# A decoder trunk on one core: K handed over behind pinned copies at the seams, one bank's copy into a free place, three of w_out's sets kept as plain sums, and the last product taken pair by pair

## The chip, the cores and the metric

The kernel runs on one core of one Trainium2 chip. Its engines are TensorE (PE, matrix products, with PEld for its weight loads), VectorE (DVE), ScalarE (ACT), GpSimd (POOL) and SyncE (SP, which issues nearly all DMAs). The metric is the time of one execution on the device, in microseconds (us); the median over runs is given. A profiled execution gives the trace, which has its own time.

## The reference

One decoder layer (DEPTH 1, BATCH 1, SEQ 2048, D_MODEL 1024, all float32), whose outputs must be met to float32-like accuracy:

```python
mod = jax.nn.silu(c) @ w_ada[l] + b_ada[l]
shift, scale, gate = jnp.split(mod, 3, axis=-1)
u = x * (1.0 + scale[:, None, :]) + shift[:, None, :]
h = u @ w_in[l]
q, k, v, a_gate, p_in, p_gate, m_a, m_p = jnp.split(h, offsets, axis=-1)
a = sliding_window_sink_attention(q, k, v, sinks[l], bias, mask) * jax.nn.silu(a_gate)
a = a @ w_attn_proj[l]
p = jnp.einsum('bsgc,gcd->bsgd', multiscale_causal_pool(p_in), w_pool_mix[l]).reshape(B, S, POOL_WIDTH)
p = (p * pool_scale[l]) * jax.nn.silu(p_gate)
p = p @ w_pool_proj[l]
y = jax.nn.sigmoid(m_a) * a + jax.nn.sigmoid(m_p) * p
y = (y @ w_out[l]) * (1.0 + gate[:, None, :])
x = layer_norm(DEEPNORM_ALPHA * x + y, ln_gain[l], ln_bias[l])
```

The attention has 16 query heads and 2 key-value heads of 64, a window of 128 and a sink per head; the pool takes causal means over 2, 4, 8 and 16 positions.

## The kernel before

**Products.** Every large matrix product is computed in 2 x 2 blocks with seven block products instead of eight. They are called B11, T1, T2, B21, T3, B22 and T4, after the *set* (the moving operand, 1024 x 512 sums of blocks) that each uses. The weights of a product are blocks of the stationary matrix or sums of them: a `Quad` loads four blocks into the tile `W` (places 0 to 3; place 0 holds A11) and `A22`, and GpSimd forms the sums in place (`sum1`, `mid`, `late`). To keep accuracy, each operand is split into a high and a low part in the matrix engine's 32-bit format, and a product is 12 matmuls of 128x128 by 128x512 (four steps, each of high·high, high·low, low·high). The split is a cast on ScalarE (high) and a subtraction on VectorE (low), `pair_split` for two places of `W`, `half_split` for `A22`; the results lie in the ring `w_set`, which has four places, so that two pair splits fill it.

**Groups and phases.** Two quads make a group. `front` does B11 and T1 of a quad, which accumulate in the banks a and b (`mm` in the trace); `back` does T2 (bank c, `lg`), B21 (into a), T3 (into c), B22 (into b) and T4 (into c), with copies and adds between them: u2 is a copy of a, taken before B21 accumulates there, and is added to c; p5 is a copy of b; then `b = c + p5`. `third(x)` splits the weights of T3 and B22 of quad x, and with `b22_first` (the first group after an attention) both quads' B22 come before T3. Finished banks go to a `consume` of the quad: `take_k` splits K into `kk` by eight alternating copies for each 512 columns (ScalarE high, VectorE low), `gate_quad` applies sigmoids, `attn_quad` and `pool_quad` apply gates and collect `wide` sums and y, and the w_out quads add the residual and normalize rows.

The order in time is: the first gate phase; attention of the first half of the sequence; the second gate phase; attention of the second half; then the "mix", four phases (attention projection and pool projection of each half), and last w_out with LayerNorm rows. In an attention, TensorE works through the heads while the products of the next phase's first quads (`opened`) are woven in, up to T2 of both and B21 of the first. The places where an attention ends and `back` takes over are called the **first seam** (to the second gate phase) and the **second seam** (to the mix). The third place of interest is the change from the last pool phase to w_out.

**What sets the order.** The program is written in one order, and a scheduler places the instructions on each engine; an engine executes its own list in that order. Engine handles named `act`, `dve`, `pe`, `sp`, `pool` are *pinned*: what is issued through them keeps the written order among itself. What is issued through `nc.scalar`, `nc.vector` and so on may be moved by the scheduler. A `tick` comes after every product; `hooks` hang further steps on ticks.

**Sets.** The sets of the next phase are loaded step by step while the present one runs. They lie in DRAM either as *plain sums* (two halves of 512 KB for each set), fetched into a spare buffer and split on arrival (`set_steps`: a fetch, and some ticks later the split, at the ticks of `SPLIT_AT`), or already *split* (four parts, 1 MB for each half), filled straight into place at the ticks of `PLAN`. w_out's sets are made in the second gate phase by `sums_to`, which calls `kept_parts`: a high part `k_hi`, a low part `k_lo` and two writes of 256 KB for each of four row pairs and each set.

Of the kernel before, what the change touches and what calls it, by code (L numbers as in the profile page):

```python
# [19 lines left out]
P = 128  # L20
# [39 lines left out]
def kernel(  # L60
# [49 lines left out]
    def set_store(name):  # L110
        return {n: dp.tile([2, P, 2, CH], F32, name=f"{name}_{n}") for n in set_names}

    def split_store(name):
        return {n: dp.tile([4, P, 2, CH], F32, name=f"{name}_{n}_split") for n in set_names}

    b12_d = dp.tile([2, P, 2, CH], F32, name="b12_d")
    u1_d = split_store("u1")
    wo_d = split_store("wo")
    ain0_d = split_store("ain0")
    ain_d = [set_store(f"ain{s}") for s in range(2)]  # L120
    pin_d = [set_store(f"pin{s}") for s in range(2)]
# [9 lines left out]
    def low(engine, dst, src, hi):  # L131
        engine.tensor_tensor(dst, src, as32(hi), ALU.subtract)  # L132
# [95 lines left out]
    def sums_to(ph, store, i, load, work, b12):  # L228

        b = []  # L230

        def x(r, c):
            return b[r][:, c * CH : (c + 1) * CH]

        def fetch():
            b.extend((ph.spare(), ph.spare()))
            b.reverse()
            for r in (1, 0):
                load(b[r], r)

        def sub(out, a, c):
            return lambda: pool.tensor_tensor(x(*out), x(*a), x(*c), ALU.subtract)

        todo = [(0, fetch), (3, lambda: work(b[0], 0)), (3.5, lambda: work(b[1], 1))]
        todo += [(at, sub(*z)) for at, z in (
            (7.5, ((0, 1), (0, 1), (0, 0))),
            (9, ((1, 1), (1, 1), (0, 1))),
            (10.5, ((1, 0), (1, 0), (1, 1))),
            (12, ((0, 0), (1, 1), (0, 0))),
        )]  # L250
        for at, name, z in (
            (4, "B11", (0, 0)), (4.7, "B12", (0, 1)), (5.4, "B21", (1, 0)), (6.1, "B22", (1, 1)),
            (8.5, "T1", (0, 1)), (10, "T2", (1, 1)), (11.5, "T4", (1, 0)), (13, "T3", (0, 0)),
        ):
            if b12 or name != "B12":
                split, keep = kept_parts(ph, store[name][i], lambda z=z: x(*z))
                todo += [(at, split), (at + 1, keep)]
        return sorted(todo, key=lambda t: t[0])
# [61 lines left out]
    def by_two(t):  # L320
        return t.rearrange("p (a c) -> p a c", a=2)
# [37 lines left out]
        tick()  # L359
        return a, b, None, None  # L360

    def back(ph, grp, opened, nxt, own, tick, b22_first=False):
        st = []
        for q, (a, b, c, w, *copy) in zip(grp, opened):
            p5 = ph.p("p5")
            if w is None:
                c = bank("lg")
                nc.scalar.copy(c, a)
                nc.scalar.copy(p5, b)
                w = pair_split(ph, q.second())[::-1]  # L370
                q.late()
                product(c, w[1], "T2")
            else:
                u2 = copy[0] if copy else ph.p("u2")
                if not copy:
                    nc.scalar.copy(u2, a)
                if c is None:
                    c = bank("lg")
                    product(c, w[1], "T2", True)
                nc.vector.tensor_tensor(c, c, u2, ALU.add)  # L380
                nc.scalar.copy(p5, b)
            tick()
            nc.vector.tensor_tensor(b, c, p5, ALU.add)
            if not copy:
                product(a, w[0], "B21")
            tick()
            q.consume(ph, 0, 0, a)
            st.append((q, b, c, p5))
        w = {}

        def ask(q):

            defer(1, lambda: q.load(ph, own, sp if b22_first else nc.sync, None))
            defer(3, lambda: q.sum1(nc.gpsimd))

# [12 lines left out]
        def with_b22(x):  # L408
            q, b, c, p5 = st[x]
            product(b, w[x][0], "B22")  # L410
            tick()
            q.consume(ph, 0, 1, b)

        if b22_first:
            for x in range(len(st)):
                third(x)
                with_b22(x)
            for x in range(len(st)):
                with_t3(x)
        else:  # L420
            for x in range(len(st)):
                third(x)
                with_t3(x)
                with_b22(x)
        for q in nxt[len(st) :]:
            ask(q)
        for q, b, c, p5 in st:
            w = half_split(ph, q.a22)
            product(c, w, "T4")
            tick()  # L430
            q.consume(ph, 1, 0, c)
# [9 lines left out]
            due.remove(d)  # L441
            d[2]()

    def ring(ph, groups, opened, hooks, nxt, after, b22_first=False):
# [12 lines left out]
        for gi, grp in enumerate(groups):  # L457
            pos[:] = [gi, 0]
            own = gi % 2 == 0 and gi + 1 < len(groups)
            back(ph, grp, opened, (groups + [nxt])[gi + 1], own, tick, b22_first and gi == 0)  # L460
# [24 lines left out]
    def set_steps(ph, store):  # L485


        if store["B11"].shape[0] == 4:
            return [(p, lambda n=n, h=h: fill_set(n, h, store[n])) for p, n, h in PLAN]
        raw, todo = {}, []  # L490

        def fetch(k):
            name, half = PLAN[k][1:]
            raw[k] = ph.spare()
            sp.dma_start(raw[k], store[name][half].rearrange("p a b -> p (a b)"))

        def split(k):
            name, half = PLAN[k][1:]
            split_set(name, 2 * half, by_two(raw[k]), 2, (act, dve))

        for k, at in enumerate(SPLIT_AT):
            if k < 2:
                todo.append((0, lambda k=k: fetch(k)))
            todo.append((at, lambda k=k: split(k)))
            if k + 2 < len(SPLIT_AT):
                todo.append((at, lambda k=k: fetch(k + 2)))
        return todo

    def planned(hooks, ph, store, last, pending={}):
        if last:  # L510
# [146 lines left out]
            low(nc.vector, dst[:, :, kv, HD:], vtp[:, :, kv, :], dst[:, :, kv, 0:HD])  # L657

    def take_k(s, t, kp):
        if s > 0 and t == 0:  # L660
            nc.vector.tensor_copy(kk[:, :, :, 0:P], kk[:, :, :, 2 * CH :])
        c0 = P + t * CH
        for kv in range(2):
            src = kp[kv * HD : kv * HD + HD, :]
            for half in (kv, 1 - kv):
                dst = kk[half * HD : half * HD + HD, kv, :, c0 : c0 + CH]
                nc.scalar.copy(dst[:, 0, :], src)
                low(nc.vector, dst[:, 1, :], src, kk[kv * HD : kv * HD + HD, kv, 0, c0 : c0 + CH])

    def bias_rows():  # L670
        room = cp.tile([P, 4 * D], F32, tag="set_T2", name="head_T2")
# [49 lines left out]
    def attention(ph, s, q0, nxt):  # L721
# [170 lines left out]
        for n in range(N + 5):  # L892
# [96 lines left out]
                    early_lo(x, which)  # L989
            if n in (59, 62):  # L990
                nxt_group[n // 62].mid()
            if n == 64:
                opened[0].append(nxt_group[0].w[:, 0, :])
                act.copy(opened[0][4], opened[0][0])
            for st in range(2):
                if n % U == 3 + 2 * st and (j, st) in sums:
                    pgs[j, st] = ld("pg", gates_d["pg"][s, j, st])
# [116 lines left out]
    def head(ph):  # L1114
# [113 lines left out]
        def second_pair(x):  # L1228

            o, u2 = opened[x], ph.p("u2")  # L1230
            o[2:] = bank("lg"), pair_split(ph, grp[x].second(), act, dve)[::-1], u2
            act.copy(u2, o[0])

        def more(x, name, i0, i1):
            a, b, c, w, _ = opened[x]
# [157 lines left out]
    with Pools("mix", spare=2, p=2, c=5) as ph:  # L1393
# [9 lines left out]
        for i, (groups, store) in enumerate(phases):  # L1403
# [7 lines left out]
            if i + 1 < len(phases):  # L1411
                planned(hooks, ph, phases[i + 1][1], True)
                nxt = phases[i + 1][0][0]
                after = lambda tick, nxt=nxt: [front(ph, q, tick) for q in nxt]
            else:
                for at, row in ((1, 2), (1, 3), (5, 4), (5, 5)):
                    hooks.setdefault((0, at), []).append(lambda row=row: load_z(ph, row))
            if i in (2, 4):
                ta.clear()
            if i == 3:  # L1420
# [8 lines left out]
            opened = ring(ph, groups, opened, hooks, nxt, after, i == 0)  # L1429
# [53 lines left out]
```

## Time and profile before

| | |
|---|---|
| median of 3 runs | 1770.89 us (1770.28 to 1771.1) |
| profiled execution | 1766.12 us |
| its span, first to last instruction | 1764.3 us |
| mean granted TensorE clock | 0.992 |
| instructions | 24983 |
| PE, DVE, ACT, POOL busy | 97%, 68%, 53%, 45% |
| DMA moved | 381.30 MB, mean 216 GB/s |

In a row of the timeline stand: start, duration, engine, line, operation, output<-inputs by name with shapes, count, and in brackets the idle time of that engine before the row and what ended it. A row with a count above one runs from the first of its instructions to the last. In a row of stretches stand the stretch, its length, then busy time and count of PE, PEld, DVE, ACT and POOL, then the granted TensorE clock (1.00 is full), the share of the DMA engines and GB/s. In a row of groups stand the count, the busy time, the mean ns of one and the idle time before. In a row of DMA issues stand the count, the size of each and the median us from issue to landing.

### The profile page before, as it was taken

The numbers are of one execution on the slowest core, as the hardware profiler recorded it, in microseconds if no ns is written. First come the engines' busy times: TensorE is split into PE (matmuls) and PEld (weight loads), VectorE is DVE, ScalarE is ACT, GpSimd is POOL, SyncE is SP. The second block draws the span as 40 slices with busy tenths as digits, with TensorE's granted clock in tenths as the row PEclk, the third lists the DMA queues.
The fourth block names the chain that finished last, engine by engine and source line by source line (L and its number), as shares of the span: only waits on it lengthen the run. The fifth ranks groups of instructions, "written<-read, shape, count | busy, mean of one in ns | idle before, by whom it ended". The sixth has DMA issues, their size and how long they took to land. (4 is left out here: it accounts for less than half of the span.)

```text
span 1764.3 us, 24983 instructions
## 1 busy us (share of the span) xinstructions
PE 1702.9 (97%) x8248; PEld 1428.7 (81%) x8248; DVE 1206.0 (68%) x2180; ACT 931.8 (53%) x1969; POOL 792.7 (45%) x618
## 2 busy tenths in 40 slices
PE   6899999999999998999999999999999989999996
PEld 5688888888888887888788888888888768888785
DVE  5967665655777786766655367777867586765777
ACT  4544444545777775454444377777744333423451
POOL 2145454431356567434434125456762562364542
PEclk9999999999999999999999999999999999999998
DMA  9384767743354567687777634544796585689432
GB/s 365 112 279 179 270 210 273 271 148 132 108 173 146 172 219 294 245 281 254 246 274 262 231 98 132 175 155 149 258 356 225 182 257 182 226 314 384 166 143 99
DMA packets 180609, 381.30 MB, mean 216 GB/s; under 512 B 18800, under 2 KB 39296, under 8 KB 180480
## 3 DMA queue, kind: packets, MB, share of 16 engines
q1 hardware_dynamic: 173696, 363.66, 59.2%
q0 software_dynamic: 3552, 11.56, 1.7%
q10 hardware_dynamic: 3232, 4.49, 0.9%
q8 instruction: 65, 1.06, 0.2%
q14 instruction: 64, 0.52, 0.1%
HBM read 244.35 MB, written 138.44 MB: 217 GB/s over the span
## 5 line engine op out<-in xcount | busy, mean ns | idle before, releaser
L56 PE MATMUL mm<-set_B,w_set 128*128 128x512 f32 x3240 | 801.8, 396 | 17.5 <-DVE w_set L132 8.7
L56 PEld LDWEIGHTS mm<-set_B,w_set 128*128 128x128 f32 x3240 | 604.2, 189 | 147.4 <-DVE w_set L132 15.2
L56 PE MATMUL lg<-set_T,w_set 128*128 128x512 f32 x2088 | 505.9, 392 | 14.0 <-DVE w_set L132 8.6
L56 PEld LDWEIGHTS lg<-set_T,w_set 128*128 128x128 f32 x2088 | 390.8, 188 | 103.7 <-DVE w_set L132 14.0
L132 DVE TENSOR_TENSOR w_set<-W,w_set 128x1024 fp32r<-128x1024 f32 x162 | 224.1, 1383 | 175.7 <-ACT w_set L325 171.4
L325 ACT CAST w_set<-W 128x1024 fp32r<-128x1024 f32 x162 | 169.7, 1049 | 242.4 <-PE mm L56 195.6
L56 PE MATMUL mm<-set_T,w_set 128*128 128x512 f32 x1080 | 266.2, 394 | 0.0
L56 PEld LDWEIGHTS mm<-set_T,w_set 128*128 128x128 f32 x1080 | 201.1, 189 | 41.3
L294 POOL TENSOR_TENSOR W<-W,A 128x512 f32<-128x512 f32 x56 | 82.1, 1466 | 221.7 <-DMA W<-in_win_dram 55.9
L303 POOL TENSOR_TENSOR W<-W 128x512 f32<-128x512 f32 x56 | 80.1, 1431 | 155.5 <-DVE w_set L132 143.9
L56 DVE TENSOR_TENSOR o<-pv,o 64x128 f32<-64x128 f32 x256 | 72.4, 283 | 88.3 <-ACT o L56 85.4
L56 ACT ACTIVATE L<-L,nm 128x257 f32<-128x257 f32 (+1 forms) x256 | 127.2, 498 | 9.3 <-DVE nm L56 3.9
L298 POOL TENSOR_TENSOR W<-W 128x512 f32<-128x512 f32 x56 | 88.1, 1574 | 93.8 <-DVE w_set L132 84.7
L56 DVE CUSTOM_DVE_ANT_0 L<-lg,bt,nsink 128x256 f32<-128x256 f32 (+1 forms) x256 | 111.6, 473 | 5.0 <-PE lg L56 0.8
L299 POOL TENSOR_TENSOR W<-W 128x512 f32<-128x512 f32 x56 | 88.1, 1573 | 37.3 <-DMA W<-in_win_dram 28.1
L56 POOL TENSOR_TENSOR w_set<-W,w_set 128x1024 fp32r<-128x1024 f32 x14 | 33.7, 2405 | 139.6 <-ACT w_set L56 97.0
L56 POOL TENSOR_TENSOR p<-nxt,pg 128x512 f32<-128x512 f32 x32 | 42.0, 1311 | 106.4 <-DVE sm L56 102.8
L56 ACT COPY o<-pv 64x256 f32<-64x256 f32 x128 | 47.3, 370 | 78.1 <-PE pv L56 77.3
L56 DVE TENSOR_TENSOR ptl<-pt,pth 128x512 fp32r<-128x512 f32 (+1 forms) x128 | 85.7, 669 | 1.9 <-ACT pth L56 1.7
L56 DVE TENSOR_TENSOR k_lo<-spare,k_hi 128x512 fp32r<-128x512 f32 x61 | 63.2, 1041 | 28.8 <-ACT k_hi L56 15.0
L56 PE MATMUL lg<-kk,qs 128*128 128x256 f32 (+1 forms) x512 | 80.5, 279 | 0.0
L56 ACT ACTIVATE L<-L,sm 128x256 f32<-128x256 f32 (+1 forms) x128 | 64.3, 502 | 29.4 <-DVE sm L56 29.4
(208 smaller groups left out, 2304.9 us busy)
## 6 DMA issues: line engine op xcount, KB each, us to landing
W<-in_win_dram SPq DMA_DIRECT2D x48, 512.0 KB, 5.3
w_set<-wmix_d SPq DMA_DIRECT2D x32, 512.0 KB, 5.2
W<-in_win_dram SPq DMA_DIRECT2D x34, 256.0 KB, 3.4
A<-in_win_dram SPq DMA_DIRECT2D x34, 256.0 KB, 5.0
ag_d<-sig SPq DMA_DIRECT2D x32, 256.0 KB, 3.3
pg_d<-sig SPq DMA_DIRECT2D x32, 256.0 KB, 3.7
ma_d<-sig SPq DMA_DIRECT2D x32, 256.0 KB, 3.9
mp_d<-sig SPq DMA_DIRECT2D x32, 256.0 KB, 3.8
```

The lines of the kernel that those rows point to most:

```text
L56: return lambda *args, **kw: self.tc.keep_in_program_order(op(*args, **kw))
L132: engine.tensor_tensor(dst, src, as32(hi), ALU.subtract)
L294: e.tensor_tensor(self.w[:, 1, :], self.w[:, 2, :], self.a22, ALU.add)
L298: e.tensor_tensor(x[:, 1, :], x[:, 1, :], x[:, 0, :], ALU.subtract)
L299: e.tensor_tensor(x[:, 2, :], x[:, 0, :], x[:, 2, :], ALU.subtract)
L303: e.tensor_tensor(x[:, 3, :], x[:, 3, :], x[:, 1, :], ALU.subtract)
L325: a.copy(by_two(hi), raw)
```

## The change

It has four parts.

1. **K handed over.** In the `back` of a first group after an attention, the pair's adds and p5 copies go through pinned `dve` and `act`, and the two `consume(0, 0)` calls (K's for the second gate phase, a gate's multiplication in the mix) are held until both quads' adds and B21 have been issued. In the second half of the sequence `take_k` is pinned as well.
2. **Second quad's copy.** In the attention, at step 66, the second quad's bank a is copied into place 0 of its `W` (A11's, no longer needed), as the first quad's is at step 64; before, `back` copied it into a `u2` tile. B21 of the second quad still is issued in `back`.
3. **Plain sums.** w_out's T3, B22 and T4 are kept as plain sums (one write for each row pair, no `k_hi` and `k_lo`), and are fetched and split on the way into w_out, in a `set_steps` that takes both kinds.
4. **The last group.** In w_out's last group, T3, B22 and T4 are done quad by quad, and not both T4 at the end. The loads of residual rows 4 and 5 come at tick 9, not 5.

```diff
     u1_d = split_store("u1")
-    wo_d = split_store("wo")
+    wo_d = {
+        **split_store("wo", ("B11", "T1", "T2", "B21", "B12")),
+        **{n: dp.tile([2, P, 2, CH], F32, name=f"wo_{n}") for n in ("T3", "B22", "T4")},
+    }
...
-            if b12 or name != "B12":
+            if store[name].shape[0] == 2:
+                todo.append((at, lambda name=name, z=z: put(sp, store, name, i, x(*z))))
+            elif b12 or name != "B12":
                 split, keep = kept_parts(ph, store[name][i], lambda z=z: x(*z))
...
         st = []
+        held = []
         for q, (a, b, c, w, *copy) in zip(grp, opened):
             p5 = ph.p("p5")
+            v = nc.vector
...
-                nc.vector.tensor_tensor(c, c, u2, ALU.add)
-                nc.scalar.copy(p5, b)
+                v = dve if b22_first else nc.vector
+                v.tensor_tensor(c, c, u2, ALU.add)
+                (act if b22_first else nc.scalar).copy(p5, b)
             tick()
-            nc.vector.tensor_tensor(b, c, p5, ALU.add)
-            if not copy:
+            v.tensor_tensor(b, c, p5, ALU.add)
+            if len(copy) < 2:
                 product(a, w[0], "B21")
             tick()
-            q.consume(ph, 0, 0, a)
             st.append((q, b, c, p5))
+            held.append((q, a))
+            if not b22_first or q is grp[-1]:
+                for z, r in held:
+                    z.consume(ph, 0, 0, r)
+                held.clear()
...
+        if finish_rows:
+            for x, (q, b, c, p5) in enumerate(st):
+                third(x)
+                with_t3(x)
+                with_b22(x)
+                product(c, half_split(ph, q.a22), "T4")
+                tick()
+                q.consume(ph, 1, 0, c)
+            return
...
     def set_steps(ph, store):
...
+        ahead = []
+        for at, (kept_at, name, half) in zip(SPLIT_AT, PLAN):
+            if store[name].shape[0] == 4:
+                todo.append((kept_at, lambda n=name, h=half: fill_set(n, h, store[n])))
+                continue
+            fetch_at = ahead[-2] if len(ahead) > 1 else 0 if store["B11"].shape[0] == 2 else at - 3
+            todo.append((at, lambda n=name, h=half: split(n, h)))
+            todo.append((fetch_at, lambda n=name, h=half: fetch(n, h)))
+            ahead.append(at)
+        return sorted(todo, key=lambda t: t[0])
...
     def take_k(s, t, kp):
+        copy, v = (act.copy, dve) if s else (nc.scalar.copy, nc.vector)
...
-            if n == 64:
-                opened[0].append(nxt_group[0].w[:, 0, :])
-                act.copy(opened[0][4], opened[0][0])
+            if n in (64, 66):
+                x = n // 66
+                opened[x] += [nxt_group[x].w[:, 0, :]] + [True] * (x == 0)
+                act.copy(opened[x][4], opened[x][0])
...
-                for at, row in ((1, 2), (1, 3), (5, 4), (5, 5)):
+                for at, row in ((1, 2), (1, 3), (9, 4), (9, 5)):
```

More of the change, by code (lines that the diff above doesn't have):

```diff
@@ L111, in set_store, with split_store @@
         return {n: dp.tile([2, P, 2, CH], F32, name=f"{name}_{n}") for n in set_names}
-    def split_store(name):
-        return {n: dp.tile([4, P, 2, CH], F32, name=f"{name}_{n}_split") for n in set_names}
+    def split_store(name, names=set_names):
+        return {n: dp.tile([4, P, 2, CH], F32, name=f"{name}_{n}_split") for n in names}
     b12_d = dp.tile([2, P, 2, CH], F32, name="b12_d")
     u1_d = split_store("u1")
-    wo_d = split_store("wo")
+    wo_d = {
+        **split_store("wo", ("B11", "T1", "T2", "B21", "B12")),
+        **{n: dp.tile([2, P, 2, CH], F32, name=f"wo_{n}") for n in ("T3", "B22", "T4")},
+    }
     ain0_d = split_store("ain0")
@@ L360, in front, with back @@
         return a, b, None, None
-    def back(ph, grp, opened, nxt, own, tick, b22_first=False):
+    def back(ph, grp, opened, nxt, own, tick, b22_first=False, finish_rows=False):
         st = []
+        held = []
         for q, (a, b, c, w, *copy) in zip(grp, opened):
             p5 = ph.p("p5")
+            v = nc.vector
             if w is None:
@@ L442, in run_due, with ring @@
             d[2]()
-    def ring(ph, groups, opened, hooks, nxt, after, b22_first=False):
+    def ring(ph, groups, opened, hooks, nxt, after, b22_first=False, rows=False):
         pos = [0, 0]
@@ L459, in ring @@
             own = gi % 2 == 0 and gi + 1 < len(groups)
-            back(ph, grp, opened, (groups + [nxt])[gi + 1], own, tick, b22_first and gi == 0)
+            back(ph, grp, opened, (groups + [nxt])[gi + 1], own, tick, b22_first and gi == 0, rows and gi + 1 == len(groups))
             if gi + 1 < len(groups):
@@ L485, in set_steps, with fetch, split @@
     def set_steps(ph, store):
-        if store["B11"].shape[0] == 4:
-            return [(p, lambda n=n, h=h: fill_set(n, h, store[n])) for p, n, h in PLAN]
         raw, todo = {}, []
[L492 to L507, printed above, removed]
+        def fetch(name, half):
+            raw[name, half] = ph.spare()
+            sp.dma_start(raw[name, half], store[name][half].rearrange("p a b -> p (a b)"))
+        def split(name, half):
+            split_set(name, 2 * half, by_two(raw[name, half]), 2, (act, dve))
+        ahead = []
[8 more added lines that the diff above has]
+        return sorted(todo, key=lambda t: t[0])
     def planned(hooks, ph, store, last, pending={}):
@@ L666, in take_k @@
                 dst = kk[half * HD : half * HD + HD, kv, :, c0 : c0 + CH]
-                nc.scalar.copy(dst[:, 0, :], src)
-                low(nc.vector, dst[:, 1, :], src, kk[kv * HD : kv * HD + HD, kv, 0, c0 : c0 + CH])
+                copy(dst[:, 0, :], src)
+                low(v, dst[:, 1, :], src, kk[kv * HD : kv * HD + HD, kv, 0, c0 : c0 + CH])
     def bias_rows():
@@ L1230, in second_pair @@
             o, u2 = opened[x], ph.p("u2")
-            o[2:] = bank("lg"), pair_split(ph, grp[x].second(), act, dve)[::-1], u2
+            o[2:] = bank("lg"), pair_split(ph, grp[x].second(), act, dve)[::-1], u2, True
             act.copy(u2, o[0])
         def more(x, name, i0, i1):
-            a, b, c, w, _ = opened[x]
+            a, b, c, w, *_ = opened[x]
             if name == "T2":
@@ L1428 @@
                 hooks.setdefault((-1, 7), []).append(lambda: [load_z(ph, row) for row in range(2)])
-            opened = ring(ph, groups, opened, hooks, nxt, after, i == 0)
+            opened = ring(ph, groups, opened, hooks, nxt, after, i == 0, i == 4)
 _INS = ['xt', 'xr', 'c', 'ccol', 'relT', 'wadat', 'wada', 'bada', 'win', 'wpt', 'sinks', 'mix', 'pscale', 'wap', 'wpp', 'wout', 'gain', 'lnb']
```

## The prediction

> **What bounds the kernel now.** I read the busy time of each engine first, then TensorE's idle stretches in the timeline, then the neighbours of each stretch that the change touches.
>
> ```profile
> PE 1702.9 (97%) x8248; PEld 1428.7 (81%) x8248; DVE 1206.0 (68%) x2180; ACT 931.8 (53%) x1969; POOL 792.7 (45%) x618
> ...
> 695.58 6.64 PE L56 MATMUL mm<-set_B,w_set 128*128 128x512 f32 x16 [6.28 <-ACT u L376]
> ...
> 850.56 0.73 PE L56 MATMUL lg<-set_T,w_set 128*128 128x512 f32 x2 [1.11 <-ACT w_set L325]
> ...
> 851.82 2.57 PE L56 MATMUL lg<-set_T,w_set 128*128 128x512 f32 x10 [0.53 <-DVE w_set L132]
> ...
> 869.91 2.35 PE L56 MATMUL lg<-set_T,w_set 128*128 128x512 f32 x9 [1.47 <-DVE w_set L132]
> ...
> 1438.13 4.14 PE L56 MATMUL mm<-set_B,w_set 128*128 128x512 f32 x10 [3.39 <-DVE w_set L132]
> ...
> 1633.78 2.60 PE L56 MATMUL mm<-set_B,w_set 128*128 128x512 f32 x10 [2.03 <-DVE rs L56]
> ...
> 1641.57 1.65 PE L56 MATMUL mm<-set_B,w_set 128*128 128x512 f32 x6 [1.78 <-DVE w_set L132]
> ```
>
> TensorE is busy 97% of the span and the change leaves its products as they are. So time can only come from gaps: 6.28 us at 695.58 (first seam, attention to second gate phase), 3.1 at 850 to 870 (the phase in which w_out's sums are made), 3.81 at 1633 and 1641 (w_out's first two groups). The second seam, near 1294, has no gap: there the change can only lose. The 3.39 at 1438 is not touched, but prices the clock below.
>
> **First seam, before.** The chain: T2 of the second quad ends, its bank `mm` has to be copied (u2) before B21 may accumulate there, and ScalarE reaches that copy late.
>
> ```profile
> 686.38 2.91 PE L56 MATMUL lg<-set_T,w_set 128*128 128x512 f32 x12
> ...
> 688.70 0.37 ACT L56 COPY o<-pv 64x256 f32<-64x256 f32 x1
> ...
> 691.84 3.83 POOL L56 TENSOR_TENSOR a<-a,a 128x512 f32<-128x512 f32 x3
> 692.50 0.58 ACT L667 CAST kk<-mm 64x512 fp32r<-64x512 f32 x1 [0.75 <-DVE kk L132]
> ...
> 694.93 0.59 ACT L376 COPY u<-mm 128x512 f32<-128x512 f32 x1
> ...
> 700.67 1.05 ACT L325 CAST w_set<-W 128x1024 fp32r<-128x1024 f32 x1 [3.57 <-PE mm L56]
> ```
> ```profile
> 695.58:698.00 2.42, 2.42 (x6) 1.94 (x7) 1.60 (x3) 0.59 (x1) 2.24 (x5) 0.50 1.03 401
> ...
> 700.00:701.00 1.00, 1.00 (x4) 0.80 (x3) 0.00 (x0) 0.33 (x1) 0.00 (x0) 0.50 0.37 135
> 701.00:702.00 1.00, 1.00 (x5) 0.81 (x4) 0.20 (x1) 0.98 (x2) 0.00 (x0) 0.79 0.00 0
> ```
>
> K's copies (`kk`) alternate with VectorE's and hold u2 until 694.93. B21 then runs at a granted clock of 0.50, and third(1)'s cast at 700.67 is released by its end: B22(0) starts at 700.7, of which some 0.7 us are still at half rate (0.79 in the stretch from 701). Counted at full clock it starts at 701.05.
>
> **First seam, after.** T2 ends at 686.38 + 2.91 = 689.29. The copy, now into A11's place, follows the o copy: 688.70 + 0.37 + 0.59 = 689.66. So B21(1) starts at 689.7, no longer at 695.58. But what ScalarE does next has been reordered too; its instructions there, before (`w_set` is a product's split weights, `W_6158` the second quad's raw ones, `mm_6641` the bank of b(0)):
>
> ```order
> L325 CAST w_set_6988<-W_6152 128x1024 [waits PE_49,Pool_49]
> L56 COPY o2_6916<-pv_6909 64x256 [waits PE_49]
> L667 CAST kk_3102<-mm_6640 64x512
> L667 CAST kk_3102<-mm_6640 64x512 [waits DVE_49] x3
> L381 COPY p5_6949<-mm_6641 128x512 [waits Pool_49]
> L376 COPY u2_6965<-mm_6758 128x512 [waits Activation_49]
> L1324 DMA cb_6948<-gate_d_80 128x1024 [waits DMAHW7_49,DMAHW1_49]
> L381 COPY p5_6964<-mm_6759 128x512 [waits DVE_49]
> L325 CAST w_set_7017<-W_6158 128x1024 [waits PE_49]
> ```
>
> And after, on the same engine at the same place:
>
> ```order
> L330 CAST w_set_6987<-W_6152 128x1024 [waits PE_49,Pool_49]
> L56 COPY o2_6916<-pv_6909 64x256 [waits PE_49]
> L56 COPY W_6158<-mm_6758 128x512
> L330 CAST w_set_7016<-W_6158 128x1024 [waits PE_49,Pool_49]
> L56 COPY p5_6950<-mm_6641 128x512 [waits Pool_49]
> L56 COPY p5_6956<-mm_6759 128x512 [waits Activation_49]
> L1346 DMA cb_6949<-gate_d_80 128x1024 [waits DMAHW7_49,DMAHW1_49]
> L56 CAST kk_3102<-mm_6640 64x512
> ```
>
> K has gone behind, but third(1)'s cast now stands ahead of the first pair's p5 copy, on which `mm=lg+p5` and so B22(0) depend. That cast waits for the end of B21(1), since the w_set ring has four places. On VectorE third(1)'s low half stands ahead of that add as well (next part). B22(0) therefore waits: B21(1) + cast + low + add.
>
> For these durations the second seam of before has the same four instructions:
>
> ```profile
> 1293.65 0.68 DVE L383 TENSOR_TENSOR mm<-lg,p 128x512 f32<-128x512 f32 x1
> 1294.06 6.05 PE L56 MATMUL mm<-set_B,w_set 128*128 128x512 f32 x26
> ...
> 1295.17 3.92 POOL L56 TENSOR_TENSOR a<-a,a 128x512 f32<-128x512 f32 x3
> ...
> 1296.81 1.05 ACT L325 CAST w_set<-W 128x1024 fp32r<-128x1024 f32 x1 [1.16 <-PE mm L56]
> 1297.89 2.28 DVE L132 TENSOR_TENSOR w_set<-W,w_set 128x1024 fp32r<-128x1024 f32 x1 [1.51 <-ACT w_set L325]
> ...
> 1632.51 1.21 DVE L132 TENSOR_TENSOR w_set<-W,w_set 128x1024 fp32r<-128x1024 f32 x1
> ```
>
> One product takes 1296.81 − 1294.06 = 2.75 at full clock. The low half takes 1.21 alone and 2.28 while GpSimd runs its a<-a; the first seam has the same three at 691.84 to 695.67, so I take 2.28. B21(1) ends at 689.7 + 2.75 = 692.45, cast to 693.5, low to 695.8, add 0.68: B22(0) at 696.5, after a gap of 4.0. Against 701.05 the gain is **4.55** (5.6 with 1.21).
>
> **Second seam.** VectorE before, at its end (`lg+=u2`, then the adds, then third(1)'s low half):
>
> ```order
> L383 TENSOR_TENSOR mm_12864<-lg_13085,p5_13176 128x512 [waits Activation_49]
> L380 TENSOR_TENSOR lg_13143<-lg_13143,u2_13187 128x512 [waits PE_49,Activation_49]
> L383 TENSOR_TENSOR mm_12982<-lg_13143,p5_13186 128x512 [waits Activation_49]
> L132 TENSOR_TENSOR w_set_13234<-W_12378,w_set_13233 128x1024 [waits PE_49,Activation_49]
> L561 TENSOR_TENSOR wide0_13184<-mm_12863,ga_13182 128x512 [waits DMAHW0_49,Pool_49]
> ```
>
> After:
>
> ```order
> L56 TENSOR_TENSOR lg_13024<-lg_13024,W_12311 128x512
> L135 TENSOR_TENSOR w_set_13172<-W_12317,w_set_13171 128x1024 [waits PE_49,Activation_49]
> L56 TENSOR_TENSOR mm_12803<-lg_13024,p5_13116 128x512 [waits DVE_49,Activation_49]
> L56 TENSOR_TENSOR lg_13082<-lg_13082,W_12317 128x512
> L56 TENSOR_TENSOR mm_12921<-lg_13082,p5_13122 128x512 [waits DVE_49,Activation_49]
> ```
>
> The low half has moved ahead of both adds. Before, the first add ran at 1293.65, and B22(0) followed B21(1) at 1296.81 without a gap (the row at 1294.06 runs on past it). Now: 1296.81 + 1.05 + 2.28 + 0.68 and hand-overs = 1300.85, a new gap of **4.0** (3.0 with 1.21) where there was none.
>
> **The clock after these gaps.** No row shows a gap of 4.0; its neighbours are these (granted clock third from the end of a row):
>
> ```profile
> 1438.00:1440.00 2.00, 1.87 (x6) 1.49 (x7) 0.67 (x2) 0.00 (x0) 2.00 (x2) 0.67 1.08 280
> 1440.00:1445.00 5.00, 5.00 (x19) 4.00 (x18) 3.03 (x4) 2.58 (x3) 2.80 (x3) 0.79 0.91 289
> 1633.78:1640.00 6.22, 6.00 (x24) 4.35 (x24) 4.64 (x7) 3.92 (x7) 4.90 (x4) 1.00 0.07 26
> ```
>
> After 3.39 us idle the clock lost 0.33 × 2 + 0.21 × 5 = 1.7 us; after 2.03 nothing. So each 4.0 gap costs 0 to 1.7. Part of a half-rate stretch falls into the gap itself, so I take 1.4 where it comes, and that it comes at one of the two: −1.4.
>
> [...]
>
> **w_out.** The seam from the mix's first attention phase to its pool phase already splits sets on the way, as w_out's will:
>
> ```profile
> 1358.79 0.97 PE L56 MATMUL mm<-set_B,w_set 128*128 128x512 f32 x3 [0.76 <-DVE w_set L132]
> ```
>
> Three sets are now read as six plain sums of 512 KB and split here, by six casts and six lows.
>
> ```profile
> 1603.96 1.05 ACT L325 CAST w_set<-W 128x1024 fp32r<-128x1024 f32 x1 [2.15 <-PE mm L56]
> ...
> 1609.38 2.88 PE L56 MATMUL lg<-set_T,w_set 128*128 128x512 f32 x12
> ...
> 1609.58 0.69 DVE L637 SCALAR_TENSOR_TENSOR wide<-wide,mm 128x512 f32<-128x512 f32 x1 [2.02 <-PE mm L56]
> ...
> 1612.10 2.88 PE L56 MATMUL mm<-set_B,w_set 128*128 128x512 f32 x12
> 1613.37 0.71 SPq L288 DMA_DIRECT2D A<-y_d  x1
> ...
> 1621.06 1.29 DVE L132 TENSOR_TENSOR w_set<-A,w_set 128x512 fp32r<-128x512 f32 x2
> ...
> 1627.30 1.70 POOL L294 TENSOR_TENSOR W<-W,A 128x512 f32<-128x512 f32 x1 [18.62 <-DMA A<-y_d]
> ```
> ```profile
> set_T<-wo_T_split SPq DMA_DIRECT2D x8, 1024.0 KB, 12.1
> ...
> spare<-pin_T SPq DMA_DIRECT2D x16, 512.0 KB, 4.1
> ```
>
> The gaps at 1633 and 1641 start with `A<-y_d`: issued at 1613.37, used at 1627.30, 13.9 later, behind set fills of 12.1 each. Six fills of 1 MB become 512 KB, and SyncE issues both A22 loads ahead of T4's fetches, so the 3.81 should mostly close; I leave 0.8, as the seam at 1358 has. Against it stands VectorE in the first w_out group. Before:
>
> ```order
> L132 TENSOR_TENSOR w_set_15490<-W_15301,w_set_15489 128x1024 [waits PE_49,Activation_49]
> L383 TENSOR_TENSOR mm_15382<-lg_15445,p5_15444 128x512 [waits PE_49]
> L637 SCALAR_TENSOR_TENSOR wide2_15323<-wide2_15323,mm_15381 128x512 [waits DMAHW7_49,DMAHW3_49,PE_49]
> L132 TENSOR_TENSOR w_set_15522<-W_15251,w_set_15521 128x1024 [waits Activation_49]
> L383 TENSOR_TENSOR mm_15417<-lg_15486,p5_15485 128x512 [waits PE_49]
> L132 TENSOR_TENSOR w_set_15567<-W_15301,w_set_15566 128x1024 [waits PE_49,Activation_49]
> ```
>
> After:
>
> ```order
> L657 SCALAR_TENSOR_TENSOR wide2_15261<-wide2_15261,mm_15323 128x512 [waits DMAHW7_49,DMAHW3_49,PE_49]
> L56 TENSOR_TENSOR set_B22_576<-spare_15352,set_B22_576 128x2x512 [waits DMAHW4_49,Activation_49]
> L135 TENSOR_TENSOR w_set_15479<-W_15189,w_set_15478 128x1024 [waits Activation_49]
> L56 TENSOR_TENSOR set_B22_576<-spare_15377,set_B22_576 128x2x512 [waits DMAHW6_49,Activation_49]
> L391 TENSOR_TENSOR mm_15362<-lg_15440,p5_15439 128x512 [waits PE_49]
> L135 TENSOR_TENSOR w_set_15519<-W_15239,w_set_15518 128x1024 [waits PE_49,Activation_49]
> ```
>
> Each half of set_B22, which waits for its fetch, now stands ahead of a product's weights. There are two spare buffers, so each fetch waits for the low two before it: T3's second low ends at 1603.96 + 1.05 + 1.21 (second(1)'s weights) + 1.21 = 1607.4; with fetches of 4.1 + cast 1.05 + low 1.21 each, B22's second half is ready at 1613.8 and T4's at 1620.2. Behind T4's stand three wide adds of 0.69 and A22's low of 0.65 (half of 1.29): weights at 1622.9. T4(0) is due, with a product every 2.72 (1612.10 − 1609.38), at 1609.38 + 6 × 2.72 = 1625.7. So 4.1 is hidden; fetches of 6.05, half of the 12.1 that a fill took here, give 1626.7, 1.0 late. The rows at this place are the fills, so I charge 1.0. w_out: 3.81 − 0.8 − 1.0 = **+2.0**.
>
> **The rest.** Twelve k_hi and k_lo and their writes go:
>
> ```profile
> L56 DVE TENSOR_TENSOR k_lo<-spare,k_hi 128x512 fp32r<-128x512 f32 x61 | 63.2, 1041 | 28.8 <-ACT k_hi L56 15.0
> ```
>
> 12 × 1.04 = 12.5 us of a VectorE that is 68% busy: only the 3.1 of gaps at 850 to 870 can shrink; I take **0.5** (−1 to 1.5, as these lows sit among others). K's sixteen conversions now run under B22 to T4, eleven us of products, and cost nothing while they stay ahead of T4's split.
>
> ```profile
> 1758.66 1.42 DVE L628 SCALAR_TENSOR_TENSOR wide<-wide,carry,wide 128x512 f32<-128x512 f32 x2 [0.44 <-POOL carry L624]
> ```
>
> T4 per pair in the last group can fill VectorE's idle bits before the end, such as this 0.44: **0.4**. Later load_z: nothing, it lets the sets go first.
>
> **Sum:** 4.55 − 4.0 − 1.4 + 2.0 + 0.5 + 0.4 = 2.05, about 2.0. The profiled run took 1766.12; the median of the runs, 1770.89, lies 4.77 above it, and I carry that over: **1768.9**. Both clocks halved: 1770.3; neither: 1767.5. A measurement can tell some 0.2%, 3.5 us: faster is below 1767.35, slower above 1774.4.
>
> **The rivals.**
> Small traps: neither clock falls and the lows take 1.21: 5.6 − 3.0 + 2.9 = 5.5, **1765.4**. For it: GpSimd's work may have ended by then; against it: both rows above. [...]
> No traps: the hoisted casts don't wait, B22(0) follows at 692.45, seam two is unhurt: 8.6 + 2.9 = 11.5, **1759.4**. Against it: 700.67 shows that cast released by TensorE.
> Slower, by a late set: B22's second half is fetched from 1607.4. With the 13.9 of `A<-y_d` it lands at 1621.3, cast and low to 1623.6, add and third(1)'s low to 1625.5; T3(1) is due at 1609.38 + 4 × 2.72 = 1620.3, so 5.2 late, and w_out gives −5.2 for +2.0: **1776.1**. It decides from a fetch of 8.7. For it: fills of 12.1 there; against it: spare fetches of 4.1 in the pool phase.
> It doesn't do what it says: K's conversions, merely moved, hold T4's weights instead of B21's by 2 to 4 us: **1772**.
>
> **How the numbers follow.** Forecast 0.52, small traps 0.18, no traps 0.04, late set 0.17, K comes back 0.09. Of the forecast's share about a quarter lies below 1767.35: faster 0.14 + 0.16 + 0.04 = 0.34, slower 0.17 + 0.01 = 0.18, same 0.48. The range, 1763.5 to 1775.0, leaves out no traps and most of the late set; it holds the ends of each price above.
>
> **What would show it.** Right: B21(1) directly after T2(1) at the first seam, then 3 to 4 us idle released by VectorE; such a gap also near 1297; gaps at 1633 and 1641 under 1 us. Wrong: no gap at 1297, a half clock at both seams, or TensorE waiting for set_B22 or set_T4 in w_out's first group.

## The result and the profile after

| | before | after |
|---|---|---|
| median | 1768.49 us (22 runs, 1763.82 to 1771.1) | 1771.76 us (22 runs, 1767.32 to 1774.91) |
| span of the profiled execution | 1764.3 us | 1768.3 us |
| instructions | 24983 | 24924 |

The ratio is 1.0015, with a 95% interval of 1.0008 to 1.0023: slower by 1.4 to 4.1 us. I had forecast 2.0 faster. The time is inside my range, but it moved the other way.

TensorE's main gaps in the timeline of the changed kernel (in brackets the gap and what ended it):

```profile
697.86 7.35 PE L56 MATMUL mm<-set_B,w_set 128*128 128x512 f32 x24 [3.49 <-DVE mm L56]
...
713.10 1.68 PE L56 MATMUL lg<-set_T,w_set 128*128 128x512 f32 x6 [1.08 <-DMA set_T<-u_T_split]
...
866.77 5.29 PE L56 MATMUL lg<-set_T,w_set 128*128 128x512 f32 x22 [0.95 <-DVE w_set L135]
...
1298.32 8.09 PE L56 MATMUL mm<-set_B,w_set 128*128 128x512 f32 x24 [3.84 <-DVE mm L56]
...
1614.94 3.02 PE L56 MATMUL lg<-set_T,w_set 128*128 128x512 f32 x12 [0.81 <-ACT lg L375]
...
1638.05 2.57 PE L56 MATMUL mm<-set_B,w_set 128*128 128x512 f32 x10 [0.60 <-DVE w_set L135]
...
1650.73 2.57 PE L56 MATMUL lg<-set_T,w_set 128*128 128x512 f32 x10 [1.50 <-DVE rs L56]
```

Both gaps that I had called traps are there: 6.28 became 3.49 at the first seam, and a gap of 3.84 stands at the second, where there was none. At the first seam the timeline shows the chain instruction by instruction:

```profile
690.72 0.59 ACT L56 COPY W<-mm 128x512 f32<-128x512 f32 x1
691.35 3.02 PE L56 MATMUL mm<-set_B,w_set 128*128 128x512 f32 x12 [0.45 <-ACT W L56]
...
694.24 1.04 ACT L330 CAST w_set<-W 128x1024 fp32r<-128x1024 f32 x1 [2.94 <-PE mm L56]
...
695.32 1.88 DVE L135 TENSOR_TENSOR w_set<-W,w_set 128x1024 fp32r<-128x1024 f32 x1 [2.67 <-ACT w_set L330]
...
697.12 0.69 DVE L56 TENSOR_TENSOR mm<-lg,p 128x512 f32<-128x512 f32 x1
```

Copy, B21(1), cast, low half, add, and only then B22(0) at 697.86. Stretches of the same trace show the granted clock (third number from the end) after the two gaps, and how busy the DMA engines are (second from the end):

```profile
692.00:700.00 8.00, 4.51 (x19) 3.34 (x18) 5.23 (x8) 4.54 (x7) 7.72 (x8) 0.95 1.03 413
...
699.20:702.60 3.40, 3.40 (x10) 2.63 (x9) 1.87 (x4) 0.88 (x2) 1.29 (x3) 0.50 0.91 337
...
1296.50:1299.90 3.40, 1.58 (x4) 1.30 (x5) 3.06 (x4) 0.00 (x0) 2.21 (x5) 0.50 1.04 381
1299.90:1303.30 3.40, 3.40 (x10) 2.66 (x9) 0.00 (x0) 0.00 (x0) 2.54 (x2) 0.50 1.02 398
```

After the first seam TensorE was busy at half rate for 3.40 us, which cost 1.7; after the second for 1.58 + 3.40, which cost 2.5.

**Where the time went.** Up to w_out's last group, TensorE executes its 8248 matmuls in the same order in all these kernels, so the start of the n-th can be subtracted. The table gives how much that difference grew over a stretch (us, minus is a gain against the kernel before; all from profiled executions):

| kernel | to 680 | first seam, 680 to 733 | second phase, 824 to 941 | second seam, 1291 to 1337 | w_out, 1598 to 1671 |
|---|---|---|---|---|---|
| after | 1.6 | −1.7 | −2.1 | 5.7 | −0.3 |
| e1 | 4.0 | 1.5 | −3.4 | −0.4 | −1.1 |
| e2 | 2.1 | 1.3 | −3.3 | −0.4 | −1.4 |
| e3 | 5.3 | 1.4 | −2.4 | 6.2 | −0.9 |
| e4 | 0.1 | −1.7 | −1.7 | 5.8 | 0.1 |
| e5 | 3.2 | −1.3 | −2.4 | −0.1 | −1.0 |
| e6 | −0.5 | −1.1 | −2.8 | −0.4 | −1.5 |
| e7 | −0.1 | 0.0 | −0.6 | 0.4 | −0.2 |
| e8 | 0.6 | −1.2 | −2.7 | −0.3 | −0.6 |
| e9 | −0.1 | −2.6 | −2.3 | −0.3 | −0.7 |
| e10 | 1.3 | −1.9 | −2.8 | −0.4 | −0.9 |
| e11 | −0.2 | −1.1 | −1.7 | 0.5 | 0.1 |
| e12 | 3.3 | −0.2 | −2.8 | −0.3 | −0.7 |
| e13 | 1.4 | −3.0 | −2.7 | −0.4 | −0.9 |

The first column is a stretch that no kernel here changes: it wanders from −0.5 to 5.3 between executions. The first seam is not changed in e6, e7, e8 and e11 either. It shows 0.0 in e7 and −1.1 to −1.2 in the other three. Behind one gap (6.28 us in before, 6.29 in e8 and e11) the 36 matmuls that follow took 11.17 us in before, 9.79 in e8 and 10.03 in e11. So some 1.2 us there is luck of the execution. Read against those, the changed first seam (−1.7, −1.7 and −1.3 in after, e4 and e5) gained between 0.1 and 1.7.

### The profile page after: what moved, and what is told of

Same layout as the page of the kernel before. It is cut to its first block, busy times and chain, and to the rows that moved or that the text cites. A ratio compares the mean times of both kernels' runs of the same rounds, so it can differ in the third digit from the quotient of the medians.

```text
span 1768.3 us, 24924 instructions
## 1 busy us (share of the span) xinstructions
PE 1703.6 (96%) x8248; PEld 1429.2 (81%) x8248; DVE 1204.8 (68%) x2174; ACT 930.6 (53%) x1963; POOL 790.6 (45%) x618
## 5 line engine op out<-in xcount | busy, mean ns | idle before, releaser
L56 PEld LDWEIGHTS lg<-set_T,w_set 128*128 128x128 f32 x2088 | 390.8, 188 | 106.7 <-DVE w_set L135 14.4
L56 ACT CAST pth<-pt 128x512 fp32r<-128x512 f32 (+1 forms) x128 | 73.5, 574 | 10.0
```

The costliest lines, as they stand in the source:

```text
L56: return lambda *args, **kw: self.tc.keep_in_program_order(op(*args, **kw))
```

## The experiments

Each was run in five rounds beside the kernel before; the ratios are to it. The kernel before had medians from 1766.66 to 1768.68 us beside them, so kernels of different rounds are compared by their ratios.

| | median | ratio (95%) |
|---|---|---|
| e1 adds first, both seams | 1766.43 | 0.9988 (0.9977 to 0.9998) |
| e2 e1 + fill early | 1767.56 | 0.9996 (0.9985 to 1.0006) |
| e3 after + fill early | 1773.16 | 1.0024 (1.0014 to 1.0033) |
| e4 after, mix written as before | 1769.47 | 1.0005 (0.9996 to 1.0013) |
| e5 after, copy at first seam only | 1764.82 | 0.9983 (0.9973 to 0.9993) |
| e6 before + plain sums | 1763.49 | 0.9976 (0.9967 to 0.9986) |
| e7 before + rows | 1765.12 | 0.9985 (0.9975 to 0.9995) |
| e8 before + sums and rows | 1764.07 | 0.9979 (0.9969 to 0.9989) |
| e9 e1's first seam, A22 moved | 1762.64 | 0.9973 (0.9960 to 0.9985) |
| e10 e5, A22 moved | 1761.31 | 0.9964 (0.9950 to 0.9979) |
| e11 e8, A22 moved | 1765.90 | 0.9988 (0.9975 to 1.0000) |
| e12 e9, K's second half late | 1761.74 | 0.9973 (0.9960 to 0.9985) |
| e13 e12, sigmoid late too | 1759.86 | 0.9953 (0.9940 to 0.9967) |

**e1: the adds ahead of third(1)'s split.** In the changed kernel the pinned copies and adds kept their order among themselves, but third(1)'s split, which is not pinned, went ahead of them. So here third(0)'s split is written before the pair, and third(1)'s, pinned, right behind it.

```diff
         held = []
+        first = pair_split(ph, grp[0].third())[::-1] if b22_first else None
...
-        w = {}
+        w = {0: first}
...
         if b22_first:
-            for x in range(len(st)):
-                third(x)
-                with_b22(x)
+            third(1, True)
+            for z, r in held:
+                z.consume(ph, 0, 0, r)
+            for x in range(len(st)):
+                if x < len(nxt):
+                    ask(nxt[x])
+                with_b22(x)
```

> The changed kernel, with third(0)'s weights split ahead of the pair and third(1)'s split and K's copies behind the pair's adds, at both seams. Trap theory: the gap of 3.84 at the second seam and its half clock go, so 6.5 us come back there; the gap of 3.49 at the first seam goes too, but the second half of T4's set there is filled late (it queues on SyncE behind A22, which waits for writes of the attention's a), so TensorE waits some 5 us for it in place of 1.08 and the first seam's net gain stays about 2: about 6.5 below the changed kernel, 3 below the kernel before. Rival, no such floor: about 11.5 below the changed kernel. Rival, the gaps come from elsewhere: same as the changed kernel.

Measured: 0.9988, some 5 us below the changed kernel. The second seam's loss is gone (−0.4 in the table). At the first seam B22(0) waits only 0.42, yet the stretch loses 1.5 where I had expected a net gain of 2. TensorE's later gaps there:

```profile
710.10 1.75 PE L56 MATMUL lg<-set_T,w_set 128*128 128x512 f32 x6 [1.21 <-ACT kk L56]
...
716.64 2.93 PE L56 MATMUL lg<-set_T,w_set 128*128 128x512 f32 x6 [4.79 <-DMA set_T<-u_T_split]
```

The gap came back as a wait of 4.79 for T4's set, about the 5 us that I had expected for it. SyncE's issues of before, of the changed kernel and of e1, and what it waits for in the first two (total, times, longest):

```profile
701.14 0.35 SPq L56 DMA_DIRECT2D A<-in_win_dram  x1
...
SPq L56 <- DMA ain_T<-a: 10.8, 1, 10.8
```
```profile
704.24 0.34 SPq L56 DMA_DIRECT2D A<-in_win_dram  x1
...
705.24 0.59 SPq L56 DMA_DIRECT2D set_T<-u_T_split  x1
...
SPq L56 <- DMA ain_T<-a: 11.1, 1, 11.1
```
```profile
707.12 0.35 SPq L56 DMA_DIRECT2D A<-in_win_dram  x1
...
708.12 0.59 SPq L56 DMA_DIRECT2D set_T<-u_T_split  x1
```

A22 of the next group lies where the attention's `a` lay; its load waits 11.1 us for the writes of a to land, and the fill of T4's second half stands behind it. That was so before (10.8), but TensorE came late enough not to notice. This bound on T4 is what the expectations call the floor.

**e2: e1, and the fill ahead of A22.**

```diff
-        for p, name, half in ((0, "T3", 0), (1, "T3", 1), (3, "T4", 0), (5, "T4", 1)):
+        for p, name, half in ((0, "T3", 0), (1, "T3", 1), (3, "T4", 0), (4, "T4", 1)):
```

> As e1, and the fill of the second half of T4's set in the second gate phase issued one tick earlier, ahead of the next quad's loads on SyncE. Floor theory: the wait for set_T at T4 goes, and the whole first gap is gained: 4 to 5 us below e1, about 8 below the kernel before. If the floor is not that queue: same as e1.

Measured: no better than e1, where I had expected 4 to 5 us below it. The wait for set_T went and two others came:

```profile
710.45 3.14 PE L56 MATMUL lg<-set_T,w_set 128*128 128x512 f32 x12 [3.40 <-ACT kk L56]
...
725.97 4.15 PE L56 MATMUL mm<-set_B,w_set 128*128 128x512 f32 x10 [2.21 <-DVE w_set L135]
```

So that one place in SyncE's queue is not the floor. Who holds ScalarE here shows in e9.

**e3: the changed kernel with the fill early.** Its edit is that of e2 alone.

> The changed kernel with only the fill of T4's second half one tick earlier in the second gate phase. Floor theory: the 1.08 us wait (with its interruption of the product, about 1.5) goes, no more, since the trap still holds: 1 to 1.5 below the changed kernel. Otherwise the same.

Measured 1.0024: no gain. The wait moved to T4's weights and to the next group:

```profile
714.17 3.12 PE L56 MATMUL lg<-set_T,w_set 128*128 128x512 f32 x12 [1.47 <-ACT w_set L337]
...
729.21 3.50 PE L56 MATMUL mm<-set_B,w_set 128*128 128x512 f32 x10 [2.20 <-DVE w_set L135]
```

**e4: the mix's first pair written as before.**

```diff
-                v = dve if b22_first else nc.vector
+                v = dve if b22_first and hand else nc.vector
...
-                (act if b22_first else nc.scalar).copy(p5, b)
+                (act if b22_first and hand else nc.scalar).copy(p5, b)
...
-            if not b22_first or q is grp[-1]:
+            if not (b22_first and hand) or q is grp[-1]:
```

`hand` is false in the mix.

> The changed kernel with pinned adds and copies and the held hand-over only at the first seam; at the second seam the pair is written as before. Trap theory: no gap near 1297 and no half clock, 6 us below the changed kernel, 2.5 to 3 below the kernel before. Rival, the gap there comes from the second quad's copy in A11's place: gap stays, same as the changed kernel.

Measured: 1.0005, by the ratio 1.8 us below the changed kernel with intervals that overlap, and not the 6 of the theory. The gap at the second seam stays, to the hundredth:

```profile
1297.22 3.36 PE L56 MATMUL mm<-set_B,w_set 128*128 128x512 f32 x7 [3.84 <-DVE mm L391]
```

The pins at the second seam are not what opened it. That part of my theory fell, and the rival was tried next.

**e5: the second quad's copy in A11's place at the first seam only.**

```diff
-            if n in (64, 66):
+            if n == 64 or n == 66 and s == 0:
```

> The changed kernel with the second quad's copy into A11's place only at the first seam; pins and held hand-over stay at both. e4 kept the gap at the second seam without the pins, so theory: it is the early copy that lets the scheduler set third(1)'s split ahead of the pair's adds there. Then no gap near 1297 and no half clock: 6 us below the changed kernel, 2.5 to 3.5 below the kernel before. Rival, the pins alone also cause it: gap of 3 to 4 stays, same as the changed kernel.

Measured: 0.9983, by the ratios 5.7 us below the changed kernel. With the pins kept and the copy gone, the seam runs through, and on VectorE both adds stand ahead of third(1)'s low half:

```profile
1293.31 8.77 PE L56 MATMUL mm<-set_B,w_set 128*128 128x512 f32 x36
```
```profile
1293.68 0.70 DVE L56 TENSOR_TENSOR mm<-lg,p 128x512 f32<-128x512 f32 x1
...
1295.63 0.70 DVE L56 TENSOR_TENSOR mm<-lg,p 128x512 f32<-128x512 f32 x1 [0.65 <-ACT p L56]
...
1297.14 2.29 DVE L135 TENSOR_TENSOR w_set<-W,w_set 128x1024 fp32r<-128x1024 f32 x1 [0.81 <-ACT w_set L330]
```

So at the second seam the early copy did it: with it, pinned or not (e4), the scheduler sets third(1)'s split ahead of the adds. Which edit does so at the first seam was not tested alone.

**e6, e7, e8: the third and the fourth part on the kernel before.** Their edits are those hunks of the change.

> The kernel before with only the third part: w_out's T3, B22 and T4 as plain sums. By the traces of the changed kernel and e1: the second gate phase gains 2 to 3 (gaps at 850 and 870), the seam to w_out about 0.5 to 1: 2.5 to 4 below the kernel before. Rival, those gaps moved only because the first seam did: within 1 of the kernel before.

> The kernel before with only the fourth part: T4 per quad in the last group, rows 4 and 5 loaded four ticks later. My forecast's term: 0.4 below the kernel before. Rival: the last rows' normalization is not shortened and the later loads make VectorE wait: 0 to 0.5 above.

> The kernel before with the third and fourth part, both seams as before. If the parts add: the sum of e6 and e7, 3 to 4 below the kernel before, and lower than e1, since e1's first seam loses about 2 by its trace. Rival, the first seam's change does gain on the median: above e1.

Measured: 0.9976, 0.9985 and 0.9979. The plain sums gain 4.2 us by the ratio (2.5 to 5.8), a little above the upper end of what was expected; in e6 the gaps at 850 are gone and 0.39 is left of the 1.47:

```profile
865.01 5.28 PE L56 MATMUL lg<-set_T,w_set 128*128 128x512 f32 x22 [0.39 <-DVE w_set L135]
...
1606.26 3.03 PE L56 MATMUL lg<-set_T,w_set 128*128 128x512 f32 x12 [0.45 <-ACT lg L373]
...
1629.05 2.60 PE L56 MATMUL mm<-set_B,w_set 128*128 128x512 f32 x10 [0.18 <-DVE w_set L135]
...
1641.89 2.56 PE L56 MATMUL lg<-set_T,w_set 128*128 128x512 f32 x10 [1.62 <-DVE rs L56]
```

e7 came out 2.7 us faster (0.9 to 4.4), more than either reading, but on top of e6 the rows add nothing (e8). From the start of the last matmul to the end, the traces take 14.4 and 14.6 us without the fourth part (before, e6), 13.5 to 14.0 in ten kernels with it and 14.7 to 14.8 in three, the changed kernel among them. What the fourth part is worth stays open.

**e9, e10, e11: A22 in memory that `a` did not use.** One line moves it; e9 has e1's order and e5's copy, e10 is e5 and e11 is e8 with it.

```diff
...
+        ph.t.tile([P, CH], F32, tag="A22", bufs=2, name="A22")
         q0 = second_phase(ph, opened, *gates1)
```

> e1's order at the first seam (adds ahead of third(1)'s split), the second quad's copy only there, and the next group's A22 given memory that the attention's a does not use, so that its load and T4's fill behind it do not wait for the writes of a. Floor theory: the 4.8 us wait for set_T at T4 in e1 goes; seam 1 gains 4 to 6 net of the kernel before instead of losing 1.5, less 1 to 3 if T4's weights then wait behind K's conversions: 3 to 6 below e1 and e5, 1760 to 1763. Rival, the DMA rate itself is the floor: no better than e1 and e8.

> e5 (the changed first seam with its gap of 3.5, second seam without the early copy) and A22 in the other memory. Floor theory: the wait for set_T near 713 goes, 1 to 2 us below e5; the gap of 3.5 and its half clock stay.

> e8 (both seams as before, plain sums, rows) with A22 in the other memory: a control. Its first seam has no wait for set_T, so the same as e8; what e9 is below this is the worth of the hand-over at the first seam once nothing behind it is late: 4 to 6 by the floor theory, 0 or less if the rate of the DMAs is the floor.

Measured: 0.9973, 0.9964 and 0.9988. In e10 the wait for set_T is gone and the trap's gap stays, as expected (first row). The control e11 does not differ from e8 (0.9979) beyond the intervals. e9 lies 2.6 us below e11 by the ratios, with intervals that overlap, between the 4 to 6 of the floor theory and the nothing of its rival. In e9 the whole seam runs as one row of three products, and then T4 waits after all; the third row is ScalarE's:

```profile
697.55 8.63 PE L56 MATMUL mm<-set_B,w_set 128*128 128x512 f32 x24 [3.49 <-DVE mm L56]
```
```profile
689.65 8.53 PE L56 MATMUL mm<-set_B,w_set 128*128 128x512 f32 x36 [0.44 <-ACT W L56]
...
704.60 0.60 ACT L565 ACTIVATE sig<-mm 128x512 f32<-128x512 f32 x1 [5.04 <-DMA ain_T<-a]
...
707.46 4.70 PE L56 MATMUL lg<-set_T,w_set 128*128 128x512 f32 x12 [3.85 <-ACT kk L56]
```

The wait is put down to `kk`, but ahead of it ScalarE stood 5.04 us in a sigmoid whose buffer also lies in a's old memory: the same writes of a, by another queue. SyncE, too, issues nothing for 12.85 us in e9 (693.08 to 705.93), but now behind the fill, ahead of a load for w_out's sums.

**e12 and e13: K's second half, then the sigmoid too, behind the splits of T4's weights.** e12 holds quad 0's finished B22 alone, e13 both quads'.

```diff
-            q.consume(ph, 0, 1, b)
+            if not hold:
+                q.consume(ph, 0, 1, b)
...
             for x in range(len(st)):
                 with_t3(x)
+            ready = [half_split(ph, q.a22) for q, *_ in st]
+            for q, b, *_ in st:
+                q.consume(ph, 0, 1, b)
```

> e9, and K's second half (the conversions from bank b) handed over behind the splits of T4's weights. Theory: the 3.85 us that TensorE waits for ACT kk ahead of T4 in e9 go, the half clock after it too, and nothing else is late: the first seam gains 3 to 5 more than in e9, 3 us below it, 1758 to 1761. Rival: the wait moves once more, to the next group's weights or banks near 710 to 725: same as e9.

> e12, and the second quad's finished B22 (a sigmoid whose buffer waits for the attention's writes of a) also handed over behind the splits of T4's weights. If the writes of a are the bound: TensorE's wait of 3 to 4 us at T4 goes, the first seam gains 4 to 6 net, 2 to 3 us below e9 and e12 on the median. If K's conversions are: the wait at T4 stays. If only moved once more: a wait of 2 us or more at the next group's first products.

Measured: 0.9973 and 0.9953. e12 is no better than e9: K was out of the way and T4 still waited, behind the sigmoid; in e13 the sigmoid's wait is gone, and what is left is the set itself:

```profile
708.15 0.60 ACT L568 ACTIVATE sig<-mm 128x512 f32<-128x512 f32 x1 [5.31 <-DMA ain_T<-a]
...
710.17 3.11 PE L56 MATMUL lg<-set_T,w_set 128*128 128x512 f32 x12 [3.12 <-ACT w_set L337]
```
```profile
691.53 8.51 PE L56 MATMUL mm<-set_B,w_set 128*128 128x512 f32 x36 [0.68 <-ACT W L56]
...
694.38 0.66 SPq L56 DMA_DIRECT2D set_T<-u_T_split  x1
...
708.89 2.12 PE L56 MATMUL lg<-set_T,w_set 128*128 128x512 f32 x6 [2.05 <-DMA set_T<-u_T_split]
...
692.00:700.00 8.00, 8.00 (x37) 6.49 (x36) 6.62 (x9) 5.66 (x8) 7.54 (x7) 1.00 1.01 403
709.00:720.00 11.00, 11.00 (x46) 9.01 (x47) 10.17 (x11) 7.24 (x13) 5.08 (x4) 0.84 0.84 284
```

The fill is now issued at 694.38, eleven us earlier than in the changed kernel, and is used at 708.9, while the DMA engines are full from 692 to 700 (1.01, 403 GB/s). That their rate is the next floor is likely but not shown: moving fewer bytes there was not tried. In e13's trace the first seam gained 1.8 to 3.0 against the kernels that leave it as before, not the 4 to 6 expected. e13 has the lowest ratio of the study, 0.9953 (0.9940 to 0.9967), below both the kernel before and the changed one; its interval overlaps e10's.

## Why the prediction was wrong

The sum's gain of 2.05 became a loss of 2.3 us in the traces (3.9 in the span, less the 1.6 to 680) and of 2.7 by the ratio. Three steps of the sum failed in that direction: the clock, where 1.4 was taken and 4.2 came; the path behind B22(0), where nothing was taken and T4's set cost 1.3; and w_out, where 2.0 was taken and 0.3 came.

- **Both traps: right in place and size.** I had gaps of 4.0 and 4.0; they were 3.49 and 3.84, by the four instructions named. But I read them off the order of the finished program without asking which edit made that order. At the second seam it is the early copy (e5); the pins, which I blamed after the result, are not it (e4).
- **The clock, "at one of the two, −1.4": the term that was most mis-sized.** It fell at both, which I had named as a sign of being wrong, for 3.4 us of busy time at the first and 5.0 at the second: 1.7 + 2.5 = 4.2 instead of 1.4. I had priced a gap of 4.0 at 0 to 1.7 from two neighbours, 3.39 and 2.03; the gap of 3.84 alone cost 2.5, and a gap's length did not settle its price (last section).
- **First seam, "the gain is 4.55": right at B22(0), but it did not last.** B22(0) started 3.0 us earlier in the trace, 4.6 with the 1.6 that the stretch to 680 had lost. I followed the chain to B22(0) and counted that as time. Behind it the half clock took some 1.4 (1.7, less what before still lost there) and T4's wait for its set 1.3, so that 1.9 was left. T4 waits for its set, the set for SyncE, SyncE for the landing of a's writes, and none of that moved. In e1 B22(0) started 7.6 us earlier by the same count, and after the wait for the set 0.7 was left. The prediction named this kind of loss only for K's conversions, priced at 1772, near the time that came; that is luck, since the changed kernel's T4 waited for its set. Even in e9 the trace's label (`ACT kk`, 3.85) covered a wait for the same writes. Shown by e1, e9, e12 and e13, one wait taken away after the other.
- **w_out, +2.0: too much.** It gained 0.3 in the changed kernel, 0.6 to 1.5 in most of its relatives. w_out's T4 was not late. But T2(1) waits 0.81 for ScalarE's copy of lg, since in VectorE's order a set's split now stands ahead of the gate product that frees the bank, and a norm row's `rs` keeps 1.50 at 1650.
- **Second phase, +0.5: too little.** 2.1 here and 2.8 in e6, where the 3.1 us of gaps nearly closed; 0.6 of that came without the third part, too (e7). I took a sixth because VectorE is 68% busy on average; what counted was whose operation stood ahead of a product's weights.
- **The rows, +0.4:** not settled, as e7 and e8 disagree.
- **The base.** The profiled execution of before and the three runs shown lay 2.4 us on either side of the median of 22, and the stretch to 680 alone moved 1.6. Terms of a few tenths were below what one profiled execution carries.

Together: without the second seam's copy (e5), the same change is 3.0 us faster than the kernel before by its ratio (1.2 to 4.8). One edit for one seam turned its sign.

## What to carry to other kernels

When a wait on the critical path goes, follow the next three consumers, through each queue and each reused buffer, to the first thing that has not moved: the gain ends there. Where a scheduler orders the engines, compare the order for each edit alone, since an edit that makes something ready earlier may lift other work ahead of what you meant to speed up. And where a wait is put down to an instruction, look at what that instruction's engine was itself waiting for.

## What the runs showed of the hardware

TensorE's granted clock fell behind some of its gaps, for a time that differed from case to case. At the first seam the products after the gap, both B22, are 24 matmuls; 24 of this size took 5.60 us at a clock of 1.00 (at 1625.69 in the kernel before). Behind gaps of nearly one length they took:

| kernel | gap | the 24 matmuls behind it |
|---|---|---|
| e3 | 3.48 | 5.74 |
| after | 3.49 | 7.35 |
| e5 | 3.45 | 8.38 |
| e10 | 3.49 | 8.63 |

The granted clock behind gaps of several lengths:

| kernel, end of the gap | gap | granted clock behind it |
|---|---|---|
| before, 695.58 | 6.28 | 0.50 to 701.40, then 1.00 |
| after, 1298.32 | 3.84 | 0.50 to 1303.30, then 1.00 |
| after, 1441.53 | 3.75 | 0.50 to 1446.70, then 1.00 |
| after, 697.86 | 3.49 | 1.00 to 699.10, 0.50 from 699.20 to 702.60, then 1.00 |
| before, 1438.13 | 3.39 | 1.00 to 1438.60, 0.50 from 1438.70 to 1442.10, then 1.00 |
| e13, 708.89 | 2.05 | mean of 0.84 over 709 to 720 |
| before, 1633.78 | 2.03 | 1.00 to 1640 |
| before, 1641.57 | 1.78 | 1.00 to 1648 |
| after, 1650.73 | 1.50 | 1.00 to 1656 |

At one place of the program (1438 in before, 1441 in after), gaps of 3.39 and 3.75 were followed by 3.40 and 5.17 us of busy time at half rate; a gap of 2.03 was followed by full rate, one of 2.05 was not. What decides between such cases was not shown.
